# Output products of a two-block transformer kernel: tokens moved from the free axis to the partitions

## The chip, the cores and the metric

The kernel runs on one core of a Trainium2 chip (the chip has eight). The metric is the device time of one execution in microseconds, as the median of several runs. The profile shows one execution.

## What is computed

The reference runs 512 tokens of width 1024 through two blocks, all in float32. The first has two layers, each an attention mixer (first a compressed, selected and windowed one, "nsa"; then a sliding window with sinks, "swa") and a squared-ReLU MLP of 4096 hidden units. The second has a hybrid of pooling and gated linear attention ("hyb"), a cross attention to 256 memory tokens ("cross") and a convolutional gated MLP of 2816 hidden units ("ffn"). Cut to what matters here:

```python
for i in range(2):                                  # first block
    h = modulate(rms_norm(x, norm_g[i, 0]), sh1, sc1)
    y = mixer_i(h) @ w_out                          # [512, 1024] @ [1024, 1024]
    x = x + (1 + g1) * rms_norm(y, norm_g[i, 1])
    h = modulate(rms_norm(x, norm_g[i, 2]), sh2, sc2)
    y = squared_relu(h @ w_up) @ w_down             # 1024 -> 4096 -> 1024
    x = x + (1 + g2) * rms_norm(y, norm_g[i, 3])
x = x + hybrid(rms_norm(x)) @ w_out                 # second block
x = x + cross_attention(rms_norm(x), rms_norm(mem)) @ wo
x = x + (silu(gate) * val) @ w_down                 # gate, val: conv of rms_norm(x) @ w_up
return rms_norm(x)
```

The changed products are those into the model's width: `w_out`, `w_down` and `wo`, seven places in all, and the norms that follow each.

## The kernel before, in words

Every large product is made of three matmuls in a reduced float32 format. `split` (line 99) writes a high part by an ACT copy and the remainder by a subtraction on VectorE (DVE); `mm3` (L126) adds high by high, low by high and high by low. `wload` (L112) loads 512 KB of weights into one of three staging tiles `st` over the SyncE queue, splits them (`wh` on L100, `wl` on L101), and has 4 buffers of each part.

Activations lie feature by feature: x, y, h and the mixers' outputs `a` are eight chunks of 128 features in the partitions, by 512 tokens in the free axis. A product takes a 128x128 block of weights as the stationary operand, and the tokens move, 512 at once or a half of 256 (`HALVES`).

Each of the seven places ends in a *tail* (`tail`, L870): for the first half of the tokens the eight output chunks m are computed, then for the second half in the order 7 to 0. Chunks 5 to 7 keep their split weights; the other five are loaded and split a second time, so that a tail loads 13 weight tiles. Tails of the first block (`y_tail`: nsa, mlp0, swa, mlp1) write y and end in `residual` (L858); those of the second (`x_tail`: hyb, cross, ffn) add into x. The sum of squares of a token runs across partitions: `Ssq` squares each chunk on ACT, adds chunks on DVE or GpSimd (POOL) by a plan written by hand (`PA`, `PB`), and `reduce` (L292) sums over the partitions by matmuls with a column of ones. `rstd` (L244) turns two columns of sums into 1/rms, and `spread` (L261, L262) copies these over the partitions by matmuls. `residual` then does, for each of eight chunks, a scaling by the norm (L864), an addition to x (L865, on DVE and POOL in turn) and a second sum of squares, and `norm_chunk` (L323 to L328) writes the next stage's h.

What covers a tail's norms: those of the first half of the tokens run beside the second half's matmuls; those of the second beside the next stage's matmuls on the first half (`project_halves` for the MLPs, `project` with `keep=4` for swa, hyb, cross and ffn). In the two MLPs of the first block, `mem_keys` or `mem_values` (192 matmuls of 256 columns, or 96 of 512) stands in between. Of the MLP's four groups of 1024 hidden units, three go down without a tail: 8 chunks of 24 matmuls with all 512 tokens. The ffn goes down in groups of 8, 7 and 7 chunks of hidden units.

The order of instructions on each engine is not the program's: the framework schedules it when the kernel is built, by a simulated timeline, and on the chip each engine then runs its own list in order. PSUM has eight banks: four tagged `mm`, two `t`, two `o`.

## Time and profile before

| | |
|---|---|
| median of 3 runs (lowest to highest) | 2091.39 us (2090.79 to 2096.15) |
| the profiled execution | 2096.53 us |
| its span, first to last instruction | 2094.7 us |
| TensorE matmuls (PE) busy | 2019.6 us, 96% |
| weight loads into TensorE (PEld) busy | 1704.9 us, 81% |
| DVE, ACT, POOL busy | 1268.1, 925.7, 397.6 us |
| mean granted TensorE clock | 0.980 |
| moved by DMA | 265.98 MB, 127 GB/s |

A busy PE in these tables counts a matmul from its start to a modelled end, and the matmuls overlap; how fast they follow one another is read from counts over a stretch of time. "Busy" shares are averages over stages with different limits.

### The profile page before, as it was taken

How to read it: one execution, taken by the hardware profiler on the slowest of the kernel's cores; microseconds unless marked ns; L12 is line 12 of the kernel's file. 1: busy time of each engine (PE TensorE's matmuls, PEld its weight loads, DVE VectorE, ACT ScalarE, POOL GpSimd, SP SyncE). 2: the span in 40 equal slices, each digit the busy share in tenths (PEclk: the TensorE clock that was granted, in tenths of full speed). 3: DMA queues.
4: the chain of work that ended last, by engine and by line, in shares of the span. 5: the costliest groups of instructions: out<-in, count | busy, mean ns of one | idle time of the engine just before them, and what ended most of it. 6: DMA issues, size and time to landing. Idle time of an engine off the chain costs nothing.

```text
span 2094.7 us, 30152 instructions
## 1 busy us (share of the span) xinstructions
PE 2019.6 (96%) x11378; PEld 1704.9 (81%) x11378; DVE 1268.1 (61%) x2417; ACT 925.7 (44%) x1728; POOL 397.6 (19%) x328
## 2 busy tenths in 40 slices
PE   8989999989999998989899999999999999999998
PEld 7766665878888898867888888988899898888888
DVE  6778866675455568685742333587637576444455
ACT  5356566543323245455543232454545455333344
POOL 0302121131202126410421020263010001001010
PEclk9999999989999999999999999999999999999999
DMA  7675332525566554441323333443324243332333
GB/s 295 192 222 150 106 103 58 192 81 192 170 196 209 178 162 139 127 110 51 112 81 100 91 101 96 136 131 91 101 92 138 64 133 101 97 95 82 109 93 102
DMA packets 87218, 265.98 MB, mean 127 GB/s; under 512 B 13729, under 2 KB 18785, under 8 KB 87074
## 3 DMA queue, kind: packets, MB, share of 16 engines
q1 hardware_dynamic: 83970, 258.88, 39.6%
q10 hardware_dynamic: 1856, 2.59, 0.5%
q0 software_dynamic: 1248, 2.59, 0.5%
q8 instruction: 90, 1.47, 0.3%
q14 instruction: 54, 0.44, 0.1%
HBM read 240.49 MB, written 5.77 MB: 118 GB/s over the span
## 4 chain that ended last, share of the span: by engine, by line
PE 85%; DVE 8%; DMA 3%; ACT 2%; issue 2%; SPq 0%; ACTq 0%; POOL 0%; DVEq 0%; POOLq 0%
PE mm L130 23%; PE mm L129 23%; PE mm L131 23%; PE o L762 4%; PE t L446 3%; DVE wl L101 1%; DVE x L865 1%; DVE ntr L864 1%; PE mm L746 1%; PE o L352 1%; PE mm L747 1%; PE o L1005 1%; PE t L292 1%; DVE hL L328 1%; DVE ssqbV L315 1%
## 5 line engine op out<-in xcount | busy, mean ns | idle before, releaser
L100 ACT ACTIVATE wh<-st 128x1024 fp32r<-128x1024 f32 (+1 forms) x344 | 357.9, 1047 | 594.1 <-PE mm L130 513.2
L101 DVE TENSOR_TENSOR wl<-st,wh 128x1024 fp32r<-128x1024 f32 (+1 forms) x303 | 371.2, 1229 | 329.4 <-ACT wh L100 324.4
L130 PE MATMUL mm<-hL,wh 128*128 128x512 f32 (+1 forms) x1568 | 553.8, 355 | 5.2 <-DVE hL L328 5.1
L131 PE MATMUL mm<-hH,wl 128*128 128x512 f32 (+1 forms) x1568 | 551.1, 354 | 1.4 <-DVE wl L101 1.4
L129 PE MATMUL mm<-hH,wh 128*128 128x512 f32 (+1 forms) x1568 | 549.6, 356 | 2.1 <-ACT hH L100 0.9
L129 PE MATMUL mm<-aH,wh 128*128 128x256 f32 (+1 forms) x1272 | 411.8, 327 | 3.4 <-ACT wh L100 1.3
L131 PE MATMUL mm<-aH,wl 128*128 128x256 f32 (+1 forms) x1272 | 413.0, 326 | 0.6 <-DVE wl L101 0.6
L130 PE MATMUL mm<-aL,wh 128*128 128x256 f32 (+1 forms) x1272 | 413.4, 326 | 0.1
L130 PEld LDWEIGHTS mm<-hL,wh 128*128 128x128 f32 x1568 | 301.6, 193 | 45.2 <-DVE hL L328 6.2
L131 PEld LDWEIGHTS mm<-hH,wl 128*128 128x128 f32 x1568 | 301.1, 193 | 40.5 <-DVE wl L101 2.0
L129 PEld LDWEIGHTS mm<-hH,wh 128*128 128x128 f32 x1568 | 299.8, 193 | 42.0 <-ACT hH L100 1.6
L129 PEld LDWEIGHTS mm<-aH,wh 128*128 128x128 f32 x1272 | 240.0, 189 | 26.2 <-ACT wh L100 2.1
L131 PEld LDWEIGHTS mm<-aH,wl 128*128 128x128 f32 x1272 | 240.8, 189 | 21.6 <-DVE wl L101 1.2
L130 PEld LDWEIGHTS mm<-aL,wh 128*128 128x128 f32 x1272 | 241.1, 190 | 20.8 <-DVE aL L101 0.3
L928 POOL TENSOR_TENSOR relu<-relu 128x512 f32<-128x512 f32 (+1 forms) x78 | 102.3, 1318 | 494.2 <-ACT relu L923 478.2
L344 DVE SCALAR_TENSOR_TENSOR ad<-ad,cs 128x1024 f32<-128x1024 f32 x90 | 115.3, 1285 | 53.6 <-DMA ad<-in_ada_w_dram 53.5
L101 POOL TENSOR_TENSOR wl<-st,wh 128x1024 fp32r<-128x1024 f32 (+1 forms) x39 | 96.0, 2464 | 146.4 <-ACT wh L100 125.8
L446 PEld LDWEIGHTS t<-pack,P 128*128 128x128 f32 x436 | 46.9, 140 | 53.7 <-issue 49.8
L1342 POOL TENSOR_TENSOR fu<-fu 128x512 f32<-128x512 f32 x22 | 29.3, 1333 | 289.1 <-DVE fu L1336 287.9
L751 ACT ACTIVATE P<-P,m 128x128 f32<-128x128 f32 (+3 forms) x128 | 70.9, 556 | 29.8 <-DVE m L749 28.6
L100 ACT ACTIVATE aH<-relu 128x512 fp32r<-128x512 f32 (+1 forms) x78 | 43.1, 553 | 91.5 <-POOL relu L928 91.2
L762 PE MATMUL o<-PT,VV 128*64 128x512 f32 (+3 forms) x256 | 81.0, 454 | 0.6 <-ACT PT L441 0.6
(403 smaller groups left out, 2665.6 us busy)
## 6 DMA issues: line engine op xcount, KB each, us to landing
ad<-in_ada_w_dram SPq DMA_DIRECT2D x90, 512.0 KB, 4.6
st<-in_w_down_dram SPq DMA_DIRECT2D x74, 512.0 KB, 3.6
st<-in_w_up_dram SPq DMA_DIRECT2D x64, 512.0 KB, 3.6
st<-in_w_fup_dram SPq DMA_DIRECT2D x44, 512.0 KB, 3.6
st<-in_w_fdown_dram SPq DMA_DIRECT2D x21, 448.0 KB, 3.4
st<-in_w_nsa_dram SPq DMA_DIRECT2D x16, 512.0 KB, 9.5
st<-in_w_nsa_out_dram SPq DMA_DIRECT2D x13, 512.0 KB, 4.2
st<-in_w_swa_out_dram SPq DMA_DIRECT2D x13, 512.0 KB, 4.8
```

Source lines behind the costliest of these rows:

```text
L100: S.activation(h, src, AF.Copy)
L101: eng.tensor_tensor(l, src, f(h), op=OP.subtract)
L129: T.matmul(o, ah, bh, start=start and i == 0, stop=False, **kw)
L130: T.matmul(o, ah, bl, start=False, stop=False, **kw)
L131: T.matmul(o, al, bh, start=False, stop=stop and i == n - 1, **kw)
L292: T.matmul(self.v[:, tb:tb + 1], kc(q, tb), ones, start=first and tb == 0, stop=self.left < 2, skip_group_check=True)
L344: V.scalar_tensor_tensor(w, w, 1.0, cs, op0=OP.mult, op1=OP.mult, accum_out=mod[:, j:j + 1])
L446: T.transpose(o, i, ident[:n, :n] if n < 128 else ident)
L751: S.activation(pq, pq, AF.Exp, bias=m[:, qb:qb + 1], scale=-1.0, accum_out=d[:, qb:qb + 1])
L762: T.matmul(o[64 * u:64 * u + 64], vs[u], ps_[u], start=start, stop=stop, skip_group_check=True)
L928: G.tensor_tensor(r, r, r, op=OP.mult)
L1342: G.tensor_tensor(u, u, pend[0], op=OP.mult)
```

## The change

In the seven places (and in the groups that go down without a tail) the operands change places: a block of 128 tokens of `a` is stationary, and 512 columns of the weights move. Outputs, x and y have tokens in the partitions: four blocks tb of 128 tokens by 1024 features, each as two widths n of 512. A weight tile now holds 256 rows by 512 columns.

- `rows` (for groups without a tail, and for the MLPs' tails) goes over width, weight tile and the four token blocks, with banks `mm` for the first width and `o`, `o`, `t`, `t` for the second.
- `rows_last` (tails of nsa, swa, hyb, cross, ffn) does both widths for blocks 0 and 1 and keeps all its weight tiles (8, in ffn 6), then block 2, then block 3 from the kept tiles.
- The sum of squares of a token is now along the free axis: `mean_sq` gets it from ACT's accumulator, `rcol` makes 1/rms as a column, and the norm's factor is a scalar per partition. The coefficient of y, which varies along the free axis now, is copied over the partitions once for each tail by `along_rows`.
- `norm_T` brings the normed x back to features in the partitions: a matmul of each 128x128 block of x with a diagonal matrix of 1/rms, then the scale and shift on evacuation, and the split.
- `project_halves` and `project(keep=4)` take the first half of the tokens chunk by chunk, the second with k outermost (before: the other way round in `project`, and k outermost in both halves of `project_halves`).
- `wload` has 5 buffers of each part; the first five weight tiles of the program no longer have staging tiles of their own. The ffn's groups are 8, 8 and 6. Pools are opened anew for each tail. The output is stored by tokens. Weights and memory are laid out to suit on the host, as other arrangements of the same arrays.

Gone are `rms_bcast`, `Ssq`, `norm_chunk`, `norm_to_h`, `residual`, `tail`, `y_tail` and `x_tail`. The core of the diff:

```diff
+NW = 5
+NB = 'AVAVAVAV'
...
+        p_, bufs = (wp, NW) if extra is None else extra
...
+            steps = [(k, i) for k in range(nk) for i in range(n)]
+            if hi == 0:
+                steps.sort(key=lambda s: s[1])
+            for k, i in steps:
+                mm3(pieces[i], [(kc(ws[i][0], k), kc(ws[i][1], k), h[0][k][:, c], h[1][k][:, c])],
+                    start=k == 0 and i % 2 == 0, stop=k == nk - 1, skip_group_check=True)
...
+            for i in range(keep):
+                mm3(banks[i][:, HALVES[0]], chunk_terms(ws[i], h, HALVES[0], range(nk)))
             for k in range(nk):
                 for i in range(keep):
-                    c = HALVES[0]
+                    c = HALVES[1]
                     w = ws[i]
                     mm3(banks[i][:, c], [(kc(w[0], k), kc(w[1], k), h[0][k][:, c], h[1][k][:, c])], start=k == 0,
                         stop=k == nk - 1)
-            for i in range(keep):
-                mm3(banks[i][:, HALVES[1]], chunk_terms(ws[i], h, HALVES[1], range(nk)))
...
+    def rcol(v, n):
...
+        s, r = (tmp(k, [128, 4], bufs=4)[:, :n] for k in ("rc_s", "rc_r"))
+        S.activation(s, v, AF.Sqrt, bias=eps)
+        V.reciprocal(r, s)
+        V.scalar_tensor_tensor(s, r, -0.5, r, op0=OP.mult, op1=OP.mult)
+        V.scalar_tensor_tensor(s, v, 1e-6, s, op0=OP.add, op1=OP.mult)
+        V.scalar_tensor_tensor(r, s, 1.5, r, op0=OP.add, op1=OP.mult)
+        return r
...
+    def mean_sq(src, acc):
...
+        q = p.tile([128, 1024], F32, name=tag, tag=tag, bufs=bufs)[:, :src.shape[-1]]
+        S.activation(q, src, AF.Square, scale=1 / 32, accum_out=acc)
...
+    def norm_T(xs, Rs, h, c, a, b=None):
...
+        ds, w = [], 128 * len(xs)
+        for r in Rs:
+            d = tmp("diag", [128, 128], bufs=4)
+            V.tensor_scalar(d, ident, r, None, op0=OP.mult)
+            ds.append(d)
+        nb = 512 // w
+        for m0 in range(0, 8, nb):
+            o = mm("t")
+            for u in range(nb):
+                for i, x in enumerate(xs):
+                    T.matmul(o[:, u * w + i * 128:u * w + i * 128 + 128], kc(x, m0 + u), ds[i], start=True, stop=True)
...
+            for u in range(nb):
+                m = m0 + u
+                hh, hl, v, g = h[0][m][:, c], h[1][m][:, c], kc(o, u, w), a[:, m:m + 1]
+                if b is None:
+                    S.activation(hh, v, AF.Copy, scale=g)
+                    V.scalar_tensor_tensor(hl, v, g, f(hh), op0=OP.mult, op1=OP.subtract)
                 else:
...
+                    t = tmp("nt", [128, 256], bufs=3)[:, :w]
+                    if NB[m] == "A":
+                        S.activation(t, v, AF.Identity, bias=b[:, m:m + 1], scale=g)
+                    else:
+                        V.tensor_scalar(t, v, g, b[:, m:m + 1], op0=OP.mult, op1=OP.add)
+                    split(hh, hl, t)
...
+    def along_rows(col, t):
...
+        for u in range(2):
+            o = mm("t")
+            for m in range(4):
+                T.matmul(kc(o, m), col[:, 4 * u + m:4 * u + m + 1].to_broadcast([128, 128]), ident, start=True, stop=True)
+            S.activation(t[:, u * 512:u * 512 + 512], o, AF.Copy)
+        return t
...
-            stage = None if i < 3 else fp.tile([128, 1024], F32, name="st0", tag="st0", bufs=FIRST - 3)
-            first_w.append(wload(A["w_nsa"][i], stage=stage, extra=None if i < 4 else (fp, FIRST - 4)))
+            first_w.append(wload(A["w_nsa"][i]))
...
+    def row_terms(a, w, k, u, tb):
+        return [(kc(a[0][k], tb), kc(a[1][k], tb), kc(w[0], u, 512), kc(w[1], u, 512))]
+
+    def rows(src, a, nk, evac, done=None):
...
+        for n in range(2):
+            banks = [mm() for _ in range(4)] if n == 0 else [mm("o"), mm("o"), mm("t"), mm("t")]
+            for j in range(nk // 2):
+                w = wload(src(n, j))
+                steps = [(u, tb) for u in range(2) for tb in range(4)]
+                if j == nk // 2 - 1:
+                    steps.sort(key=lambda s: s[1])
+                for u, tb in steps:
+                    k = 2 * j + u
+                    mm3(banks[tb], row_terms(a, w, k, u, tb), start=k == 0, stop=k == nk - 1)
+            for tb in range(4):
+                evac(tb, n, banks[tb])
+                if n and done and tb % 2:
+                    done((tb - 1, tb))
+
+    def rows_last(src, a, nk, evac, done):
...
+        ws, nj, wx = {}, nk // 2, later[0]
+        banks = [[mm(), mm()] for _ in range(2)]
+        for n in range(2):
+            for j in range(nj):
+                w = ws[n, j] = wload(src(n, j), extra=(wx, 2 * nj - NW) if len(ws) >= NW else None)
+                steps = [(u, tb) for u in range(2) for tb in range(2)]
+                if j == nj - 1:
+                    steps.sort(key=lambda s: s[1])
+                for u, tb in steps:
+                    k = 2 * j + u
+                    mm3(banks[n][tb], row_terms(a, w, k, u, tb), start=k == 0, stop=k == nk - 1)
+            for tb in range(2):
+                evac(tb, n, banks[n][tb])
+        done((0, 1))
+        for tb in (2, 3):
+            for n in range(2):
+                o = mm("o")
+                for k in range(nk):
+                    mm3(o, row_terms(a, ws[n, k // 2], k, k % 2, tb), start=k == 0, stop=k == nk - 1)
+                evac(tb, n, o)
+            done((tb,))
...
+    def total(s):
+        V.tensor_tensor(s[:, 2:3], s[:, 0:1], s[:, 1:2], op=OP.add)
+        return rcol(s[:, 2:3], 1)
...
+    WIDTHS = [(slice(0, 512)), (slice(512, 1024))]
...
+    def y_last(how, src, a, nk, y, acc, x, h, cy, an, bn):
...
+        cb = along_rows(cy, tmp("along", [128, 1024], bufs=1))
+        ss = [small4() for _ in range(4)]
+
+        def evac(tb, n, o):
+            c = WIDTHS[n]
+            if not acc:
+                mean_sq(o, ss[tb][:, n:n + 1])
+                V.tensor_tensor(y[:, tb, c], o, cb[:, c], op=OP.mult)
             else:
...
+                V.tensor_tensor(y[:, tb, c], y[:, tb, c], o, op=OP.add)
+                mean_sq(y[:, tb, c], ss[tb][:, n:n + 1])
+                V.tensor_tensor(y[:, tb, c], y[:, tb, c], cb[:, c], op=OP.mult)
+
...
+        def done(tbs):
+            s2 = []
+            for tb in tbs:
+                r = total(ss[tb])
+                s2.append(small4())
+                for n, c in enumerate(WIDTHS):
+                    V.scalar_tensor_tensor(x[:, tb, c], y[:, tb, c], r, x[:, tb, c], op0=OP.mult, op1=OP.add)
+                    mean_sq(x[:, tb, c], s2[-1][:, n:n + 1])
+            norm_T([x[:, tb] for tb in tbs], [total(s) for s in s2], h, cols_of(tbs), an(), bn())
+        how(src, a, nk, evac, done)
...
+    def x_last(src, a, nk, x, then):
...
+        ss = [small4() for _ in range(4)]
+
+        def evac(tb, n, o):
+            c = WIDTHS[n]
+            V.tensor_tensor(x[:, tb, c], x[:, tb, c], o, op=OP.add)
+            mean_sq(x[:, tb, c], ss[tb][:, n:n + 1])
+        rows_last(src, a, nk, evac, lambda tbs: then(tbs, [total(ss[tb]) for tb in tbs]))
...
+                    with tail_pool():
+                        mem_norm(p, mh)
...
+                    cy = need(l, 5)
+                    with tail_pool():
+                        y_last(rows, src, a, 8, y, True, x, hn, cy, an, bn)
+                        mem(mp, mh)
...
-    GROUPS = ((0, 8), (8, 7), (15, 7))
+    GROUPS = ((0, 8), (8, 8), (16, 6))
...
+            if f0 < 16:
+                def add(tb, n, o):
+                    c = slice(n * 512, n * 512 + 512)
+                    V.tensor_tensor(x[:, tb, c], x[:, tb, c], o, op=OP.add)
+                rows(src, (ah, al), n, add)
             else:
-                x_tail(src, (ah, al), n, x, then, PF)
+                x_last(src, (ah, al), n, x, then)
...
+            cy = need(0, 2)
+            y = p.tile([128, 4, 1024], F32, name="y", tag="y", bufs=1)
+            with tail_pool():
+                y_last(rows_last, out_of("w_nsa_out"), a, 8, y, False, x, h, cy, lambda: need(0, 4), lambda: need(0, 3))
...
+        with pool("ffn") as p, tail_pool():
+            fw = along_rows(nw["final"], tmp("along", [128, 1024], bufs=1))
```

`y_last` and `x_last` are called from `whole` with `rows_last`, and from `mlp` with `rows`; `mem_norm` uses `mean_sq`, `rcol` and `norm_T`.

## Rows read from the trace of the kernel before

**Rows 1.** The page: busy time of each engine; shares of the chain by engine.
```profile
PE 2019.6 (96%) x11378; PEld 1704.9 (81%) x11378; DVE 1268.1 (61%) x2417; ACT 925.7 (44%) x1728; POOL 397.6 (19%) x328
...
PE 85%; DVE 8%; DMA 3%; ACT 2%; issue 2%; SPq 0%; ACTq 0%; POOL 0%; DVEq 0%; POOLq 0%
```

**Rows 2.** Windows without waits: length, then each engine’s busy us (instructions), PE clock, DMA.
```profile
510.00:740.00 230.00, 230.00 (x1016) 190.57 (x1015) 127.53 (x171) 70.41 (x89) 33.38 (x21) 1.00 0.60 194
...
379.00:400.00 21.00, 21.00 (x177) 21.00 (x177) 16.34 (x24) 9.46 (x19) 1.34 (x1) 1.00 0.97 359
```

**Rows 3.** The same view, four stretches around the ends of tails.
```profile
424.00:452.00 28.00, 17.93 (x98) 16.44 (x99) 24.06 (x47) 11.84 (x26) 12.78 (x10) 0.66 0.36 114
...
793.00:806.00 13.00, 9.89 (x81) 9.52 (x80) 12.66 (x17) 6.82 (x12) 9.99 (x6) 1.00 0.42 135
...
824.00:838.00 14.00, 10.19 (x76) 9.81 (x75) 12.78 (x22) 7.39 (x15) 5.95 (x5) 0.92 0.48 145
...
1012.00:1027.00 15.00, 9.13 (x59) 8.46 (x58) 13.15 (x24) 8.01 (x17) 5.25 (x3) 0.77 0.61 189
```

**Rows 4.** Longest waits of PE: 376 to 460, 760 to 860, 980 to 1060.
```profile
PE mm L130 <- DVE hL L328: 2.1, 1, 2.1
...
PE t L292 <- DVE ssqbV L315: 6.3, 2, 3.5
...
PE t L292 <- ACT sqP L307: 2.8, 1, 2.8
```

**Rows 5.** Groups by line and form: count, busy us, mean ns, idle before.
```profile
L101 DVE TENSOR_TENSOR wl<-st,wh 128x1024 fp32r<-128x1024 f32 x282 | 348.9, 1241 | 308.9 <-ACT wh L100 304.0 <-PE mm L131 4.4
...
L100 ACT ACTIVATE wh<-st 128x1024 fp32r<-128x1024 f32 x320 | 336.3, 1057 | 558.6 <-PE mm L130 480.9 <-DMA Z<-P 12.5 <-PE mm L131 9.7
...
L864 DVE SCALAR_TENSOR_TENSOR ntr<-y,coef,t 128x256 f32<-128x256 f32 x64 | 27.0, 474 | 3.6 <-PE t L262 3.6
...
L865 DVE TENSOR_TENSOR x<-x,ntr 128x256 f32<-128x256 f32 x32 | 27.6, 872 | 0.0
...
L315 DVE TENSOR_TENSOR ssqaV<-ssqaV,sqV 128x256 f32<-128x256 f32 x69 | 43.3, 628 | 13.7 <-ACT sqV L307 13.4
...
L328 DVE SCALAR_TENSOR_TENSOR hL<-nt,mod,hH 128x256 fp32r<-128x256 f32 x48 | 29.4, 631 | 0.6 <-ACT hH L327 0.5
...
L948 DVE TENSOR_TENSOR y<-y,mm 128x512 f32<-128x512 f32 x32 | 21.9, 686 | 71.7 <-PE mm L131 71.7
...
L946 ACT ACTIVATE y<-mm 128x512 f32<-128x512 f32 x16 | 9.2, 578 | 0.0
...
L751 ACT ACTIVATION_READ_ACCUMULATOR P<-P,m 128x1 f32 x128 | 24.2, 189 | 0.0
...
L254 DVE SCALAR_TENSOR_TENSOR rs_s<-rs_h 128x2 f32<-128x2 f32 x26 | 9.6, 374 | 0.6
```

**Rows 6.** The chain, 1498 to 1512 and 228 to 240: start, us, what.
```profile
1498.51 1.79 PE mm L1186 x16
...
230.94 1.02 PE t L446 x8
```

**Rows 7.** Windows over the span for L292 alone, then for L261 alone.
```profile
0.00:2095.00 2095.00, 23.41 (x164) 23.55 (x164) 0.98 0.41 127
...
0.00:2095.00 2095.00, 16.98 (x64) 13.06 (x64) 0.98 0.41 127
```

**Rows 8.** Line L865: duration ns min/median/max of its DVE instructions.
```profile
L865 DVE TENSOR_TENSOR x<-x,ntr x32: 410/952/2616, 411.9 to 1413.2; 128x256 f32<-128x256 f32 x32
```

**Rows 9.** DMA issues: the page; then 0 to 70 us: KB, us to landing.
```profile
st<-in_w_nsa_out_dram SPq DMA_DIRECT2D x13, 512.0 KB, 4.2
...
st<-in_w_nsa_dram SPq DMA_DIRECT2D x8, 512.0 KB, 10.2
```

**Rows 10.** Timeline of the end, DVE and the output’s DMA queue.
```profile
2084.58 0.42 DVE L909 TENSOR_TENSOR x<-x,mm 128x256 f32<-128x256 f32 x1 [1.15 <-PE mm L131]
...
2089.11 2.12 SPq L1439 DMA_DIRECT2D out_dram<-fin  x4
```

More of the change, by code (lines that the diff above doesn't have):

```diff
@@ L38 @@
 PG = ((0,), (1, 3), (2,))
-RT = "too"
 SG, SG1 = (0, 1), (0, 1)
@@ L110, in bg, with wload @@
             bg_queue.pop(0)()
[L112 to L114 removed]
+    def wload(src, n=1024, eng=V, extra=None):
+        st = wp.tile([128, 1024], F32, name="st", tag="st", bufs=3)
+        p_, bufs = (wp, NW) if extra is None else extra
         h = p_.tile([128, 1024], F32R, name="wh", tag="wh", bufs=bufs)
@@ L262, in spread, with tail_pool @@
         T.matmul(o, rl[:, j:j + 1].to_broadcast([128, 128]), identr, start=False, stop=True)
-    def rms_bcast(ssq, tag="t"):
-        rh, rl = rstd(ssq.v[:, :2], 2)
-        R = mm(tag)
-        for tb in range(2):
-            spread(kc(R, tb), rh, rl, tb)
-        return R[:, :256]
-    later = []
+    later, sq_pool = [None], [None]
+    @contextmanager
+    def tail_pool():
+        with pool("tail") as later[0]:
+            yield
     def tmp(tag, shape, dt=F32, bufs=2):
         return later[0].tile(shape, dt, name=tag, tag=tag, bufs=bufs)
-    SB, SQ, NT, NTR = {"a": 1, "b": 1}, 1, 3, 6
@@ L384, in mem_norm @@
     def mem_norm(p, mh):
-        sq = Ssq()
-        ts = []
+        ts, rs = [], []
         for i in range(2):
-            t = p.tile([128, 1024], F32, name="memt", tag="relu", bufs=3)
-            Q.dma_start(t, A["memT"][:, 4 * i:4 * i + 4].rearrange("p a t -> p (a t)"))
-            ts += [kc(t, m, 256) for m in range(4)]
-        for m in range(8):
-            sq.add(ts[m])
-        norm_to_h(ts, rms_bcast(sq), mh, slice(0, 256), nw["mem"])
+            t = p.tile([128, 1024], F32, name="relu", tag="relu", bufs=NR)
+            Q.dma_start(t, A["mem"][i])
+            ss = tmp("ss", [128, 4], bufs=12)
+            mean_sq(t, ss[:, :1])
+            ts.append(t)
+            rs.append(rcol(ss[:, :1], 1))
+        norm_T(ts, rs, mh, slice(0, 256), nw["mem"])
     def mem_keys(p, mh):
@@ L870, in tail @@
-    def tail(src, a, nk, each, after, j0=0):
-        held = {}
-        for hi, c in enumerate(HALVES):
-            for m in (range(8) if hi == 0 else reversed(range(8))):
-                w = held.pop(m) if m in held else wload(src(m), nk * 128, eng=G if (hi, m) in TG else V)
-                if hi == 0 and m >= 5:
-                    held[m] = w
-                b = mm(cols=256)
-                mm3(b, chunk_terms(w, a, c, range(nk)))
-                each(hi, c, m, b)
-            after(hi, c)
+    def row_terms(a, w, k, u, tb):
+        return [(kc(a[0][k], tb), kc(a[1][k], tb), kc(w[0], u, 512), kc(w[1], u, 512))]
@@ L1364, in whole, with to_h, out_of @@
         xp = ctx.enter_context(pool("x"))
-        later.append(xp)
-        x = xp.tile([128, 8, 512], F32, name="x", tag="x")
+        x = xp.tile([128, 4, 1024], F32, name="x", tag="x")
+        def to_h(hn, w):
+            return lambda tbs, rs: norm_T([x[:, tb] for tb in tbs], rs, hn, cols_of(tbs), w)
+        def out_of(name):
+            return lambda n, j: A[name][n, j]
         with pool("mlp0") as p, pool("mlp0_a") as pa:
-            ada_pool[:] = [p, 3, "relu"]
+            ada_pool[:] = [p, NR, "relu"]
+            sq_pool[0] = p, "relu", NR
             a = ([], [])
-            y = p.tile([128, 8, 512], F32, name="y", tag="y", bufs=1)
             for m in range(6):
@@ L1407, in whole @@
             h = hn
-        def to_h(hn, w):
-            return lambda c, R: norm_to_h([x[:, m, c] for m in range(8)], R, hn, c, w)
-        with pool("hyb") as p:
+        sq_pool[0] = None
+        with pool("hyb_a") as pa:
             a = ([], [])
-            hybrid(h, p, a)
+            with pool("hyb") as p:
+                hybrid(h, p, pa, a)
             h = new_h()
-            x_tail(lambda m: A["w_hyb_out"][m], a, 8, x, to_h(h, nw["xattn"]))
-        with pool("cross") as p:
+            with tail_pool():
+                x_last(out_of("w_hyb_out"), a, 8, x, to_h(h, nw["xattn"]))
@@ new lines, in whole, with finish @@
+            with tail_pool():
+                x_last(out_of("w_xo"), a, 8, x, to_h(h, nw["ffn"]))
+        with pool("ffn") as p, tail_pool():
+            fw = along_rows(nw["final"], tmp("along", [128, 1024], bufs=1))
+            def finish(tbs, rs):
+                for tb, r in zip(tbs, rs):
+                    for c in WIDTHS:
+                        V.scalar_tensor_tensor(x[:, tb, c], x[:, tb, c], r, fw[:, c], op0=OP.mult, op1=OP.mult)
+                        Q.dma_start(out[tb * 128:tb * 128 + 128, c], x[:, tb, c])
@@ L1504, in prep @@
     rows = np.concatenate([(g * 4 + k) * 64 + np.arange(64) for k in range(4) for g in range(4)])
-    A["w_nsa_out"] = chunks(i["nsa_w_out"][0][rows])
+    A["w_nsa_out"] = halves(i["nsa_w_out"][0][rows])
     A["cmp_pe"] = i["nsa_cmp_pe"][0].reshape(2, 2, 16, 64).transpose(1, 3, 0, 2).reshape(128, 2, 16)
@@ L1521, in prep @@
     A["w_up"] = np.concatenate([chunks(w) for w in i["mlp_w_up"]])
-    A["w_down"] = np.concatenate([chunks(w[g * 1024:(g + 1) * 1024]) for w in i["mlp_w_down"] for g in range(4)])
+    A["w_down"] = np.stack([halves(w[g * 1024:(g + 1) * 1024]) for w in i["mlp_w_down"] for g in range(4)])
     ws = i["swa_w_in"][0]
```

248 lines of the change are left out of this document (70 added, 178 removed).

## The prediction

> **What bounds the kernel now.** I read the page first: PE is busy 96% of the span and makes 85% of the chain, DVE 8% [rows 1]. So the time is TensorE's, and two things can change it: how many matmuls follow one another at which pace, and where PE stands still. Busy time cannot tell these apart, since it counts overlapping matmuls; so I took windows in which nothing waits. From 510 to 740 us all matmuls have 512 columns; the count takes in the two that straddle the edges, which leaves 1014 in 230 us, 0.2268 us each. From 379 to 400 all have 256: 175 in 21 us, 0.1200 us each [rows 2]. Two narrow ones cost 0.2400, one wide one 0.2268: a narrow pair pays 0.0132 us more for the same columns.
>
> Then I looked for PE's gaps, at the ends of tails. At the narrow pace the 98 matmuls from 424 to 452 need 11.8 us of 28: 16.2 lost, at a granted clock of 0.66, which mixes the two levels of 1.2 and 2.4 GHz. In the same way 81 matmuls leave 3.3 lost of 13 us, 76 leave 4.9 of 14, and 59 leave 7.9 of 15 [rows 3]. Sum 32.3 us: the first window is the nsa tail, the next two mlp0's, the last swa's. The waits name DVE or ACT's squares as the last to come: a late hL, sums of squares that the matmuls with ones wait for [rows 4]. In the first window DVE is busy 24.06 us of 28, so there it is the bound behind PE [rows 3]. Part of its load is contention: the addition on L865 takes 0.41 us at best and 0.95 in the median, while POOL does the same work beside it [rows 8].
>
> **The change, part by part.** *Merging.* A tail does 8 chunks x 8 k x 3 terms x 2 halves = 384 narrow matmuls; six tails and ffn's 8 x 7 x 3 x 2 = 336 make 2640. They become 1320 wide ones, the shift of a chunk of hidden units between ffn's groups included. 1320 x 0.0132 = 17.4 us less [rows 2]. The groups without a tail keep 192 wide matmuls, 24 per weight tile.
>
> The Trainium skill, page "TensorE: Matmul & The Clock Gate", section "Back-to-back issue gap", gives 262 cycles for 256 columns and 518 for 512 at full clock, so that merging a pair would save 2.5 ns; by that the 1320 pairs would give an estimated 3.3 us, not 17.4. The trace disagrees: its pair differs by 13.2 ns [rows 2].
>
> *Small matmuls.* Gone: 164 with a column of ones, and three quarters of the 64 + 64 that spread 1/rms (the gated attention keeps 16 + 16), 96 [rows 7]. New: `norm_T`, 32 for each of six tails and 16 for each of two memory norms, 224, and `along_rows`, 5 x 8 = 40. A float32 matmul of 128 columns takes 1.79/16 = 0.112 us [rows 6], so the new ones cost 29.6. The old ones: 164 between 0.112 and 0.143 (23.41/164), 96 at 0.112: 29.1 to 34.2. Net +0.5 to -4.6; I take 0, since ones in a wait cost nothing.
>
> The skill's page "Perfetto Trace Analysis", section "Transposes", speaks against `norm_T`: a transposition should use TensorE's transpose, not a standard matmul. Here standard ones take 0.112 us and the attention's transposes 1.02/8 = 0.128 [rows 6], so the trace does not bear a price out, and 224 of them would cost nothing extra.
>
> *Weights.* Tails load 8 tiles instead of 13, ffn 6 instead of 13: 37 fewer, each 1.06 us of ACT, 1.24 of DVE (POOL in some) and one DMA of 512 KB (448 in ffn) [rows 5, 9]. `rows_last` uses up a tile in 12 x 0.2268 = 2.7 us in its first phase; DVE at 1.24 and ACT at 1.06 keep up, so these are worth nothing to PE there, only room on DVE beside the norms.
>
> *The norms.* For one tail of `residual` DVE had 16 scalings (0.474), 8 additions (0.872), 17 sums (0.628), 16 `nt` at the 0.474 of their like, 16 `hL` (0.631), four chains of 1/rms (about 1.5 at the mean 0.374 of their small steps, taken for all four) and 11 weight splits: 62.5 us [rows 5]. After: 8 splits 9.9; 16 operations of 512 columns at 0.686 = 11.0; 8 chains 12; 8 diagonals, not shown, between nothing and the 0.474 of a 256-column operation, say 2; for h, 12 operations of 256 columns at 0.631 and 24 of 128 at no more than 0.474, 18.9. Sum 54, or 44 if 128 columns and small steps take half. POOL loses its 8 additions and its sums altogether, so DVE's rest runs less beside it. A seventh to a third less DVE work, in fewer steps one after another.
>
> Coverage, `rows_last`: blocks 2 and 3 take 2 x 48 x 0.2268 = 21.8 us after blocks 0 and 1 are out. Their norm is some 15 us of DVE and ACT, so h's first half should stand when PE needs it. After the last matmul, block 3's chain is some 11 us: evacuation and square 0.69 + 0.77 (ACT 0.578 + 0.189), 1/rms 1.5, x 1.4, square 0.77, 1/rms 1.5, diagonal 0.4, h 8 x 0.474 [rows 5]. The next stage's first half covers it: 7 x 24 x 0.12 = 20.2 us in the MLPs, 4 x 24 x 0.12 = 11.5 in hyb and cross. If that cover were gone it would cost 11 us a tail. `rows`: in the MLPs' tails all four blocks end within the last 4 us, so both norms, some 35 us of DVE, come after; 23 us of `mem_keys` and 11.5 of swa's first half stand over them. There I expect waits to remain.
>
> How much of the 32.3 us goes? Nothing, if the scheduled places of the new matmuls are as early as the old ones' were; all, if DVE's room decides. I take three quarters, 24 us: DVE was nearly full where PE waited [rows 3], a sixth to a third of its work goes, and waits shrink by more than the work does.
>
> *The end.* The last output's addition starts at 2084.6 and the span ends at 2094.7; the four stores are issued from 2089.1 over 2.12 us, so the end stands some 3.5 us behind the last issue [rows 10]. After: 0.69 + 0.77 + 1.5 + 2 x 0.69 + 0.6 for handing on + 3.5 = 8.4 us in place of 10.1: 1.7 less.
>
> *Start and buffers.* Without staging of their own, the fourth and fifth weight loads wait on SyncE for a split; the loads there land 10.2 us after issue [rows 9], so a queue stands before the DMA engines that hides some 4 us of blocking. 0; if that cover were gone, those 4 us. A fifth buffer: 0 to a few us of gain in the nsa stage; 0. `mean_sq` borrows a `relu` buffer in the MLPs, where ada's loads stand in line too: at most one DVE step of 1024 columns, 1.24 us [rows 5], on no path.
>
> **The sum.** -17.4 + 0 - 24 - 1.7 = -43 us. The profiled execution took 2096.5, which gives 2053.5; it lies 5.1 us above the median of the runs shown, so against that median: 2048 us.
>
> **The rivals.** *Waits unchanged:* the diagonal matmuls stand in PE's list where the ones and spreads stood, and each waits for DVE the same way. For it: most of PE's named waits are at such matmuls [rows 4]. Against: DVE's smaller load. 2091.4 - 17.4 - 1.7 = 2072 us.
>
> *No waits left:* the 32.3 us and smaller ones that I did not add up, some 10, all go: 2091.4 - 17.4 - 1.7 - 42 = 2030 us. Against it: the MLPs' tails.
>
> *The MLPs' tails eat it:* 35 us of DVE at the contended pace, 0.95 for 0.41 [rows 8], would be past 60, and each of two tails would wait some 20 us in place of 4.1 (mlp0's 8.2 over two). With three quarters of the other 24.1 gone: -17.4 - 1.7 - 18 + 40 - 8.2 = -5, 2086 us, no change. Against: POOL is busy for only part of that stretch, 5.95 us of 14 in the later window [rows 3].
>
> *Slower, by held weights:* `rows_last` holds all its tiles until block 3 has used them, and the next stage's splits are put behind block 3's norm on DVE. Then PE waits 11 + 1.06 + 1.24 = 13.3 us at each of four tails (nsa, swa, hyb, cross), where it waited 24 in all: -17.4 - 1.7 - 24 + 53 = +10, 2101 us. It decides from 10.8 us a tail. Against it: the tiles of the first width come free from 9.5 us before the end, one every 1.36.
>
> *The merge gives nothing:* if wide matmuls with a new stationary block each go at two narrow ones' pace, 0.240, the time is 2048 + 17.4 = 2065. Against: the wide ones of now have a new block each too [rows 2]. By the skill's page above it would be an estimated 2062.
>
> **How the numbers follow.** Chances: my sum 0.52, waits unchanged 0.20, none left 0.15, the MLPs' tails 0.05, held weights 0.06, merge 0.02. The range of 2024 to 2078 takes in the first three with their bounds and the last, and leaves out the tails' and the held weights' cases and some of the edges. Within 0.3% (6 us) is about what a measurement of this kernel cannot tell from no change. Faster: 0.52 + 0.20 + 0.15 + 0.02 = 0.89; same 0.05; slower 0.06. The likeliest case alone: 2040 to 2058.
>
> **What would show it.** The tails' matmuls at 0.2268 us, and 13 x 512 KB down to 8 for each weight. No window of 28 us with 16 lost behind the nsa tail. PE's waits at `norm_T`'s matmuls and at hL, in the MLPs' tails most. DVE's instructions of 0.95 gone. The prediction is wrong if PE waits for `wl` at the start of the stages after `rows_last`, or if the lost time behind the tails sums to over 20 us again.

## The result, and the profile after

The changed kernel takes 2126.6 us (median; 2125.3 to 2130.0) where the kernel before took 2091.1: ratio 1.017, 95% interval 1.0146 to 1.0193. It is 35 us slower; 43 us faster was forecast. The profiled execution took 2125.3 us, its span is 2123.2 (before 2094.7), so the two traces have 28.5 us between them.

The page of the changed kernel: span, busy times, chain by engine.

```profile
span 2123.2 us, 27619 instructions
...
PE 2035.6 (96%) x10326; PEld 1666.9 (79%) x10326; DVE 1161.2 (55%) x2322; ACT 905.3 (43%) x1740; POOL 306.4 (14%) x243
...
PE 86%; DVE 6%; ACT 3%; DMA 3%; issue 2%; ACTq 0%; SPq 0%; DVEq 0%; POOL 0%
```

Against [rows 1] DVE has 107 us less to do and POOL 91 less, as the change promised; PE has 1052 records fewer and is busy 16 us longer. What grew on PE is seen by groups, PE alone, forms apart:

```profile
L433 PE MATMUL t<-pack,P 128*128 128x128 f32 x436 | 75.7, 289 | 2.3 <-DVE PT L430 0.8 <-ACT PT L428 0.6 <-POOL P L532 0.4
...
L298 PE MATMUL t<-diag,x 128*128 128x128 f32 x384 | 52.0, 285 | 9.9 <-DVE diag L291 9.9
...
L318 PE MATMUL t<-pack,coef 128*128 128x128 f32 x64 | 8.8, 281 | 0.0
L298 PE MATMUL t<-diag,relu 128*128 128x128 f32 x64 | 8.4, 274 | 0.0
```

`norm_T`'s L298 stands with 384 + 64 = 448 records, and the program issues 224 such matmuls; `along_rows`'s L318 has 64 and, for the norms' weights, 16 (not shown) for 40. **A float32 matmul is two records**, each 0.112 us from its start to the next. The prediction counted the new ones by instructions and the old ones by records. The line that it took the price from holds the same pair: L1186's 16 records in 1.79 us [rows 6] are 8 matmuls of the program (`heads`), so 0.224 us each.

Stage by stage, from the first matmul of a stage to the first of the next (worked out from the starts of PE's matmuls in the two traces):

| stage | before | after |
|---|---|---|
| nsa; its tail | 376.4; 59.0 | 380.6; 49.3 |
| mlp0, first group; rest and tail | 56.0; 347.3 | 63.4; 345.6 |
| **swa**; its tail | **114.5**; 68.4 | **127.5**; 69.3 |
| mlp1, first group; rest and tail | 54.8; 336.2 | 56.6; 342.0 |
| hyb; its tail | 137.1; 46.3 | 130.4; 48.5 |
| cross; its tail | 66.7; 53.5 | 70.8; 56.9 |
| **ffn, first up group**; rest | **89.6**; 288.9 | **99.2**; 282.9 |

Of the four tails that stand alone only nsa's is shorter, by 9.7 us, and the group behind it loses 7.4 of these again: before, PE stood mostly ahead of that group's first matmul (435.4 us), now it stands inside the group. The greatest losses are in two stages *behind* a tail, swa and ffn's first group. PE's waits in the changed kernel (total us, times, longest):

```profile
PE mm L124 <- ACT wh L95: 14.6, 4, 10.1
PE t L298 <- DVE diag L291: 9.9, 4, 3.7
PE mm L124 <- ACT vf L1089: 6.4, 1, 6.4
PE o L124 <- DVE y L914: 4.8, 1, 4.8
PE mm L1060 <- DMA hq<-rBL: 4.7, 1, 4.7
...
PE mm L124 <- DVE fu L1369: 3.8, 1, 3.8
```

The first stands at 445 us in mlp0's first group (10.1 of the 14.6), the third at 865 in swa, the fourth at 1014 in swa's tail, the last one shown at 1769 in ffn. None of these four is at `norm_T`, where I expected them; [rows 4] had named hL and sums of squares. The waits for `diag` are at `norm_T`, in the two MLPs' tails; with those for `wh`, which stand at the starts of mlp0 and mlp1, they make 24.5 us. Windows (length, each engine's busy us, PE clock): two inside tails, then the wait of 445, what follows the one of 865, and the one of 1014.

```profile
386.00:416.00 30.00, 30.00 (x132) 24.53 (x131) 9.02 (x31) 8.69 (x24) 0.00 (x0) 1.00 0.01 4
...
2083.00:2113.00 30.00, 30.00 (x131) 24.10 (x130) 13.91 (x32) 8.87 (x21) 1.29 (x1) 1.00 0.13 48
...
442.00:457.00 15.00, 3.92 (x30) 3.43 (x28) 11.19 (x27) 9.19 (x23) 4.20 (x5) 0.77 0.32 106
...
872.20:877.30 5.10, 5.10 (x15) 3.96 (x13) 5.10 (x7) 1.02 (x2) 3.26 (x2) 0.55 0.72 201
...
1013.00:1020.00 7.00, 2.17 (x8) 1.44 (x7) 5.75 (x23) 4.59 (x15) 0.00 (x0) 0.76 0.01 4
```

The end, DVE's last block:

```profile
2115.93 0.69 DVE L937 TENSOR_TENSOR x<-x,o 128x512 f32<-128x512 f32 x1 [3.50 <-PE o L126]
...
2118.77 1.42 DVE L1471 SCALAR_TENSOR_TENSOR x<-x,rc_r,along 128x512 f32<-128x512 f32 x2
```

From 2115.9 to 2123.2 it takes 7.3 us, where [rows 10] had 10.1.

### The profile page after: what moved, and what is told of

Its sections match the earlier page's. It is cut to its first block, busy times and chain, and to the rows that moved or that the text cites. A ratio compares the mean times of both kernels' runs of the same rounds, so it can differ in the third digit from the quotient of the medians.

```text
span 2123.2 us, 27619 instructions
## 1 busy us (share of the span) xinstructions
PE 2035.6 (96%) x10326; PEld 1666.9 (79%) x10326; DVE 1161.2 (55%) x2322; ACT 905.3 (43%) x1740; POOL 306.4 (14%) x243
## 4 chain that ended last, share of the span: by engine, by line
PE 86%; DVE 6%; ACT 3%; DMA 3%; issue 2%; ACTq 0%; SPq 0%; DVEq 0%; POOL 0%
PE mm L124 18%; PE mm L126 18%; PE mm L125 18%; PE o L124 4%; PE o L125 4%; PE o L126 4%; PE o L748 3%; PE t L433 3%; PE t L298 2%; DMA ad<-in_ada_w_dram 2%; PE t L124 2%; PE t L125 2%; PE t L126 2%; PE mm L732 1%; ACT wh L95 1%
## 5 line engine op out<-in xcount | busy, mean ns | idle before, releaser
L96 DVE TENSOR_TENSOR wl<-st,wh 128x1024 fp32r<-128x1024 f32 x273 | 341.2, 1254 | 455.2 <-ACT wh L95 454.6
L95 ACT ACTIVATE wh<-st 128x1024 fp32r<-128x1024 f32 x307 | 320.8, 1053 | 554.4 <-PE mm L125 248.2
L124 PE MATMUL mm<-hH,wh 128*128 128x512 f32 (+1 forms) x1456 | 523.4, 361 | 25.7 <-ACT wh L95 14.6
L124 PE MATMUL mm<-wh,aH 128*128 128x512 f32 x444 | 173.9, 393 | 3.9 <-ACT aH L95 3.9
L125 PE MATMUL mm<-wl,aH 128*128 128x512 f32 x444 | 174.2, 392 | 0.0
L126 PE MATMUL mm<-wh,aL 128*128 128x512 f32 x444 | 171.9, 392 | 0.0
L124 PE MATMUL o<-wh,aH 128*128 128x512 f32 x284 | 113.1, 398 | 4.8 <-DVE y L914 4.8
L125 PE MATMUL o<-wl,aH 128*128 128x512 f32 x284 | 113.0, 398 | 0.0
L126 PE MATMUL o<-wh,aL 128*128 128x512 f32 x284 | 112.2, 395 | 0.0
L124 PEld LDWEIGHTS mm<-wh,aH 128*128 128x128 f32 x444 | 83.5, 188 | 22.2 <-ACT aH L95 4.1
L126 PEld LDWEIGHTS mm<-wh,aL 128*128 128x128 f32 x444 | 83.6, 188 | 18.1
```

The costliest lines, as they stand in the source:

```text
L95: S.activation(h, src, AF.Copy)
L96: eng.tensor_tensor(l, src, f(h), op=OP.subtract)
L124: T.matmul(o, ah, bh, start=start and i == 0, stop=False, **kw)
L125: T.matmul(o, ah, bl, start=False, stop=False, **kw)
L126: T.matmul(o, al, bh, start=False, stop=stop and i == n - 1, **kw)
```

## The experiments

All times are medians, "before" is the kernel before, run beside each; ratios are against it, with 95% intervals. Edits are to the changed kernel unless said. Two limits hold for all of them. In these sessions the kernel before took 2089.4 to 2093.6 us, so a difference of under some 4 us between two experiments says nothing. And each edit makes the framework schedule the whole program anew: the time to the first matmul of nsa's tail, ahead of every edit, is 376.8 to 386.5 us in the experiments' traces, so that one trace's stage shows a cause only where a wait comes or goes with it.

**1. `project`'s old order of steps.** The kernel before with the new order, and the changed kernel with the old one:

```diff
+            for k in range(nk):
+                for i in range(keep):
+                    c = HALVES[0]
...
-            for i in range(keep):
-                mm3(banks[i][:, HALVES[0]], chunk_terms(ws[i], h, HALVES[0], range(nk)))
-            for k in range(nk):
-                for i in range(keep):
-                    c = HALVES[1]
...
+            for i in range(keep):
+                mm3(banks[i][:, HALVES[1]], chunk_terms(ws[i], h, HALVES[1], range(nk)))
```

> The changed kernel with one piece put back: in `project` with held weights (swa's, cross's and ffn's first four chunks) the first half of the tokens goes k by k over all four chunks and the second half chunk by chunk, as before the change. Theory 1 (the change's new order lets all four chunks end at once, so that their banks and weights come free together: PE stands 6.7 us at 865 us and 5.1 at 885 in swa, 2.8 in cross, 3.9 in ffn's first group, and runs at the lower clock behind each): 10 to 20 us less than the changed kernel's 2126.6, so 2106 to 2117. Rival (the second half of h comes so late after the new tails that the old order waits for it instead): within 4 us of 2126.6, with new waits for hH or hL in those stages.

> The kernel before with one piece of the change: `project` with held weights takes the first half chunk by chunk and the second half k by k over all four. Theory 1 (this order lets banks and weights come free all at once, whatever the tail in front): 8 to 20 us more than 2091, so 2099 to 2111, with a PE gap of several us behind the four chunks in swa and in ffn's first group. Rival (the gap comes from the new tails in front, not from the order): 2088 to 2095.

Measured 2107.2 us (1.008; 1.0058 to 1.0101), 19.4 less, and in the kernel before 2113.7 (1.0108; 1.0081 to 1.0135), 22 more. Both go as theory 1 has it, the second 3 us beyond its range. In the first one's trace swa takes 116.6 us and ffn's first up group 93.7, which is 10.9 and 5.5 less. Waits of PE in the kernel before with that one edit:

```profile
PE mm L129 <- ACT vf L1056: 6.4, 1, 6.4
...
PE mm L129 <- DVE fu L1336: 3.8, 1, 3.8
```

They are the 6.4 and 3.8 us of the changed kernel, with the old tails in front. With k outermost in the second half the four chunks end together; their banks, and the weights for the next chunks, come free only then. That the order is a loss by itself is shown; that ending together is all of the reason is not (see the mixed order in experiment 7).

**2. Transposes for diagonal matmuls.**

```diff
-            V.tensor_scalar(d, ident, r, None, op0=OP.mult)
+            S.activation(d, s, AF.Copy, scale=Rs[i])   # or V.tensor_scalar, in turn; s: 256 columns of x
...
-                    T.matmul(o[...], kc(x, m0 + u), ds[i], start=True, stop=True)
+                    transpose(o[...], chunk(i, m0 + u))
```

> The changed kernel with norm_T's diagonal matmuls replaced: each block of x is multiplied by its 1/rms first (pieces of 256 columns, ACT and VectorE in turn), and TensorE's transpose turns it. Theory 1 (each of the 224 float32 matmuls of norm_T stands in the trace as two records of 0.112 us and costs 0.224; a transpose is one record of about 0.10): 224 x 0.12 = 27 us less for PE, of which some 5 are lost again to the 64 scalings of 256 columns, so 2100 to 2112. Rival (the small matmuls stand in waits and cost nothing, the loss is all in waits): 2122 to 2135, the scalings lengthen the chains.

2099.7 us (1.0042; 1.0024 to 1.0059), 26.9 less, 0.3 us past the near end of theory 1's range. The 224 are one record each now:

```profile
L441 PE MATMUL t<-pack,xn 128*128 128x128 f32 x224 | 34.7, 279 | 10.9 <-DVE nt L318 5.4 <-DVE rc_s L278 4.2 <-DVE xn L298 1.0
```

**3. Every diagonal matmul twice** (`for _ in range(2):` around it).

> The changed kernel with every diagonal matmul of norm_T issued twice into the same place. Theory 1 (0.224 us each, on PE's path): 224 x 0.224 = 50 us more, less what falls into waits, so 2162 to 2178. Rival (0.112 each, as the prediction had it): 25 more at the most, 2140 to 2152. Rival (they stand in waits): under 10 more.

2159.4 us (1.0323; 1.0298 to 1.0348): 32.8 more. That lies between the first two expectations: above the 25 that 0.112 us each could cost, and short of the 50 of 0.224. Its trace, of the longest of its five runs, has 448 records more (50.2 us at 0.112) and a span 45.1 us longer; some of them fall into waits. By its interval the median alone does not exclude 25. With the run before, and with the starts in the changed kernel's trace (448 records at a mean distance of 0.111 us for 224 matmuls), the price is 0.224.

**4. Squares in a buffer of their own, 5. other places for weights, 6. other banks.**

```diff
-        p, tag, bufs = sq_pool[0] or (later[0], "sq", 1)
+            q = later[0].tile([128, 512], F32, name="sq", tag="sq", bufs=1)
```

> The changed kernel with the 512-column squares of mean_sq in a buffer of their own (in the tail's pool), so that ada's loads no longer share the three relu buffers with them. Theory A for the 10.4 us that PE stands at 445 us, in the stage behind the nsa tail (ada's seven loads, held up by the squares, put their products on VectorE into the middle of block 3's norm): ada's loads go back into the tail and that stage loses 5 to 10 us, so 2116 to 2122. Theory B (PE waits there for three weights whose place in memory was the tail's pool, so that their splits stand behind the whole norm): the gap stays, 2123 to 2130.

```diff
+            lastw[0] = es.enter_context(pool("lastw")) if last else None
...
-        ws, nj, wx = {}, nk // 2, later[0]
+        ws, nj, wx = {}, nk // 2, lastw[0] or later[0]
```

> The changed kernel with the three last weights of rows_last in a pool of their own, opened ahead of the tail's other temporaries, in the two tails that an MLP follows. The three extra weights of the MLP's first stage then lie where those weights lay, and not on the norm's temporaries. Theory B (those three weights' splits wait for the last reader of the tail's pool): they go ahead of block 3's norm, the gap of 10.4 us at 445 us goes, and so do the 2.3 and 1.7 us at 1051: 8 to 16 us less, 2111 to 2119. Theory A (VectorE's ada products): within 4 us of 2126.6.

```diff
-                o = mm("o")
+                o = mm("o") if tb == 2 else mm()
```

> The changed kernel with block 3's sums in rows_last in the four banks of the first blocks, and only block 2's in the two others. Theory (the 5.2 us that PE stands at 1014 us, in the swa tail, is block 3's first matmul waiting for the bank of block 2, whose reader on VectorE stands behind the norm of blocks 0 and 1): the gap goes, 3 to 7 us less, 2120 to 2124. Rival (PE waits a little later for the same norm instead): 2125 to 2131.

(`ada` stands for the products that make the modulation's coefficients; they are computed for the most part on DVE, from weights of their own.) Squares: 2110.9 us (1.0095; 1.0073 to 1.0118), 15.7 less, more than expected; mlp0's first group loses 6.8. Places: 2114.5 (1.0106; 1.0083 to 1.0128), 12.2 less; that group loses 7.8. So both theories on the 10.1 us at 445 hold in part: each remedy closes most of that wait, and neither theory's claim that the other's remedy does nothing holds. ACT's timeline shows the second. In the changed kernel the splits of the weights that PE waits for stand behind the last reader of block 3's norm:

```profile
444.27 0.46 ACT L308 ACTIVATE nt<-t,mod,coef 128x128 f32<-128x128 f32 x1 [2.69 <-PE t L298]
...
453.65 0.31 ACT L95 ACTIVATE hH<-nt 128x128 fp32r<-128x128 f32 x1 [0.53 <-DVE nt L310]
453.87 0.40 ACT L95 ACTIVATE aH<-relu 128x256 fp32r<-128x256 f32 x1
454.17 1.99 ACT L95 ACTIVATE wh<-st 128x1024 fp32r<-128x1024 f32 x2
```

With the weights in other places they go ahead of it, 20 us earlier:

```profile
433.70 2.94 ACT L95 ACTIVATE wh<-st 128x1024 fp32r<-128x1024 f32 x3
436.55 0.28 ACT L276 ACTIVATE rc_s<-ss,eps 128x1 f32<-128x1 f32 x1
436.98 0.46 ACT L310 ACTIVATE nt<-t,mod,coef 128x128 f32<-128x128 f32 x1 [0.16 <-PE t L300]
```

The rest of the squares' gain lies mostly in swa, 127.5 to 121.2 us, where the wait for `hq` falls from 4.7 to 2.5; why is open. Banks: 2119.3 (1.0127; 1.01 to 1.0154), 7.3 less, though the intervals still touch; the wait for `y` L914 is gone, and swa's tail falls from 69.3 to 62.9 us, of which the first group of mlp1 takes 2.4 back.

**7. Remedies together:** the old order with transposes; then all five; then all five with a mixed order (second half k by k up to k = 4, then chunk by chunk); then all five with `project_halves` k by k in its first half too (its `steps.sort` left out).

> The old order of `project` with held weights and the transposes together (the first and second experiments). If the two causes are separate, their gains add up: 2126.6 - 19.4 - 26.9 = 2080, 2075 to 2085, below the kernel before (2091). If the transposes' shorter stay on PE only uncovers the same waits, 2090 to 2100.

> All five remedies on the changed kernel: transposes, the old order of `project` with held weights, squares in their own buffer, rows_last's last weights in their own pool, and block 3's sums in other banks. If the causes are separate except for the two that close the same gap at 445 us: 2082.6 - 14 (to 16) - 7 = 2060, 2054 to 2068, below the kernel before by 1 to 2 per cent and near the prediction. If PE's waits only move on to the next late operand: 2070 to 2083.

> As the run with all five remedies, but `project` with held weights keeps the new order of its first half, and its second half goes k by k over four chunks only up to k = 4 and then chunk by chunk. If what counts is that the chunks end one after the other: within 4 us of that run. If the late second half of h counts too: up to 8 us faster than it.

> As the run with all five remedies, and `project_halves` (the MLPs' first seven chunks) gets back the order before the change as well: k by k over all seven chunks in the first half too. If that order needs all seven weights at its start, the stages behind the nsa and swa tails wait for splits: 3 to 10 us more than that run. If the new order there was a loss like the one of `project`: 2 to 6 us less.

Two: 2082.6 us (0.9954; 0.9939 to 0.9969), they add up. Five: 2074.4 (0.9926; 0.9911 to 0.9941), 52 less than the changed kernel, while one by one they save 82. The gap at 445 is counted twice in the 82, and PE now waits longer elsewhere: for `wh` at the start of mlp1 (6.4 us, in the changed kernel 3.4) and for `hL` at the start of mlp0:

```profile
PE mm L125 <- ACT wh L96: 6.4, 2, 5.3
PE mm L126 <- DVE hL L97: 5.8, 1, 5.8
```

Mixed: 2087.6 (0.999; 0.9979 to 1.0002), 13 worse. There the chunks end one after the other, 9 matmuls of 0.12 us apart, so ending in turn by that much is not enough, and what else in the order costs is open; PE waits 4.3 us for `vf` in swa again. Halves: 2073.7 (0.9921; 0.9905 to 0.9938), no difference, neither expectation holds.

**8. The merge alone taken back:** each wide matmul of the tails as two narrow ones; on the changed kernel, and on the one with five remedies.

```diff
+        for c in HALVES:
+            mm3(o[:, c], [t[:2] + (t[2][:, c], t[3][:, c]) for t in terms], ...)
```

> The changed kernel with the merge alone taken back: in the six tails and ffn's last group each matmul of 512 columns is issued as two of 256, 1296 more in all, at the same places. By the prediction's term (two narrow ones 0.2400 us, a wide one 0.2268): 1296 x 0.0132 = 17.1 us more than the changed kernel's 2126.6, so 2140 to 2147. Rival (a pair costs 2.5 ns more, as the page on the clock gate has it): 3 us more, 2127 to 2133.

> As the run with all five remedies (2074.4), with the merge taken back: 1296 more matmuls, each of 512 columns issued as two of 256. On the changed kernel the same edit cost 0.8 us where 17.1 were expected. Theory (what PE saves by the merge it waits for behind the tails, whose ends VectorE and ACT set): again little, 2074 to 2081. Rival (on the changed kernel the waits that the remedies took away hid the slower matmuls; without them the merge shows its worth): 10 to 17 us more, 2084 to 2092.

2127.4 us (1.0182; 1.0167 to 1.0197): 0.8 us, no measurable difference from the merged one. With the remedies 2084.3 (0.9959; 0.9940 to 0.9979) against 0.9926: 0.33%, 7 us, with intervals that touch. The price differs from place to place. The narrow kernel's window in ffn's tail, beside the changed one's 2083 to 2113 above:

```profile
2085.00:2115.00 30.00, 30.00 (x259) 30.00 (x258) 13.21 (x32) 8.21 (x20) 1.29 (x1) 1.00 0.14 54
```

By their starts, narrow ones follow one another there at 0.1172 us, wide ones at 0.2332: a pair costs 1.2 ns more, not 13.2. That is the cheapest place. Worked out in the same way from the two traces, where nothing waits at full clock, a pair costs 4.7 ns more in swa's tail, 8.1 to 9.5 in nsa's, hyb's and cross's, and 12.5 in the MLPs': 11 us over the 1296 pairs. With the remedies it is 12, of which 7 show in the time. On the changed kernel nearly all of it goes into waits and clock: distances more than 0.5 us beyond the usual one of their shape sum to 83.9 us in the changed kernel and 75.2 in its narrow version, and the mean granted clock is 0.975 against 0.982. Whether the wide matmuls bring these waits, or another schedule of the build does, is not shown.

**9. 1/rms left out of the tails**, on the same two kernels.

```diff
-        V.tensor_tensor(s[:, 2:3], s[:, 0:1], s[:, 1:2], op=OP.add)
-        return rcol(s[:, 2:3], 1)
+        return rk
```

> The changed kernel with 1/rms left out of the tails: `total` gives a constant column, so that the sum of the two squares, the root and the four small steps behind each go, twice a block; squares, scalings, diagonals and matmuls stay. Theory (PE's waits behind the tails hang on this chain): of the 46 us of waits and slow matmuls in the stages of the nsa, mlp0, swa and mlp1 tails and behind them 15 to 30 go, 2097 to 2112. Rival (they hang on the places of weights, on banks and on what stands ahead in ACT's and VectorE's lists): at most 8 go, 2118 to 2128.

> The same with the five remedies, which leave 43 us of waits and slow matmuls in those stages. Theory (with places, banks and orders mended, the chain of 1/rms is what PE waits for): 15 to 30 us less than 2074.4, 2044 to 2059, the prediction's number. Rival: at most 8 less, 2066 to 2076.

What is left out is not the 1/rms chain alone: nothing waits for the squares any more either, and these two kernels do not compute the tails' norms, so that 2048.5 being the forecast's number is chance. 2092.2 us (0.9994; 0.9975 to 1.0013), 34 less, beyond the theory's range, and 2048.5 (0.9789; 0.9751 to 0.9826), 26 less, inside it. In each, 2.0 of these are at the program's end. In the changed kernel without 1/rms the waits at `diag` are gone, those at `wh` are down to 0.4 us, and those of swa's and ffn's order stay:

```profile
PE mm L124 <- ACT vf L1090: 6.4, 1, 6.4
PE mm L1061 <- DMA hq<-rBL: 4.7, 1, 4.7
...
PE mm L124 <- DVE fu L1370: 3.8, 1, 3.8
```

**10. Links of that chain:** root and reciprocal without the refinement's three steps (`V.reciprocal(r, s)`, then `return r`); one chain for two blocks (two columns at once); both, with experiment 7's `project_halves`.

> The kernel with all five remedies, and in the tails' 1/rms the three small steps behind the reciprocal (the refinement) left out: root and reciprocal alone. Leaving out the whole chain of 1/rms took 26 us from that kernel. Theory (each link of the chain counts by its length; three of its six links, 0.17 us each with the same again in hand-over): 8 to 16 us less than 2074.4, 2058 to 2066. Rival (the sum over the squares and the hop to ACT for the root make the wait, not VectorE's small steps): at most 5 less.

> The kernel with all five remedies, and one chain of 1/rms for the two blocks of a pair (two columns at once) instead of one each: five chains fewer of each kind of norm where pairs end together. Theory (VectorE's many small steps delay what stands behind them): 3 to 8 us less than 2074.4, 2066 to 2071. Rival (the first block of a pair now waits for the second): no change or up to 5 more, 2073 to 2080.

> Both of these, with the old order of `project_halves` as well. If they add: 12 to 22 us less than 2074, 2052 to 2062, the fastest of all runs that compute the whole.

2069.9 us (0.9899; 0.9869 to 0.9928), 2072.7 (0.9915; 0.9884 to 0.9945), 2071.1 (0.9923; 0.9895 to 0.9951), against 2074.4 (0.9926): the intervals overlap. The first two fit their rivals (the second misses its by 0.3 us), and the gains do not add. The refinement is at most a small part of what PE waits for, and DVE's load is not it: without the refinement DVE is busy for 1154.9 us in place of 1183.4, 28.5 less, for 4.5 us of time; without the whole chain it is 1146.7, 36.7 less, for 26 (pages of the kernels with five remedies, without the refinement, without the chain):

```profile
PE 1999.2 (97%) x10102; PEld 1629.5 (79%) x10102; DVE 1183.4 (57%) x2350; ACT 925.6 (45%) x1796; POOL 309.9 (15%) x243
...
PE 1996.5 (97%) x10102; PEld 1626.6 (79%) x10102; DVE 1154.9 (56%) x2206; ACT 926.5 (45%) x1796; POOL 307.6 (15%) x243
...
PE 1995.5 (98%) x10102; PEld 1625.4 (79%) x10102; DVE 1146.7 (56%) x2131; ACT 911.4 (45%) x1749; POOL 309.1 (15%) x243
```

Which of the other links it is (the squares on ACT, the sum, the hop to ACT for the root) stays open.

## Why the prediction was wrong

The two spans differ by 28.5 us, where the sum said -43. Of the 71.5 between them the small matmuls make 30, the waits some 36, the merge some 6; the end goes 1 the other way.

**The small matmuls, "I take 0": this step failed.** Old ones: 164 x 0.112 + 96 x 0.112 = 29.1 us, counted in records. New ones: 264 x 0.112 = 29.6, counted in instructions, of which each has two records: 528 x 0.112 = 59.1. Net +30.0. Experiments 2 and 3 show it on the chip. The price was misread where it was taken: [rows 6] has 16 records for 8 matmuls. The Trainium skill's page "Perfetto Trace Analysis", section "Transposes", had the right of it; I set it aside by comparing one of two records (0.112) with the one record of a transpose. The Trainium skill's page "FP8 and Floating Point Precision", section "TensorE Precision Notes", says that true float32 makes four passes; the trace agrees: 0.224 us is 3.95 times the 0.0567 that 128 of the 512 columns of a wide fp32r matmul take at 0.2268.

**The waits, "three quarters of 32.3 go": this step failed too, its sign was wrong.** The spans differ by 28.5 = 30.0 for small matmuls, less 11 for the merge (experiment 8), less 2.8 at the end, plus the waits and what goes with them: some +12 in place of -24. Measured directly, by the starts as in experiment 8, the waits grew from 70.5 to 83.9 us between the two traces. One of the prediction's signs of being wrong, over 20 us lost behind the tails, is there with the 24.5 us for `wh` and `diag`; the other, a wait for `wl` at a stage's start, showed as one for `wh`. Four steps made this up:
- *"DVE's room decides."* DVE lost 8% of its work and PE still waits. Taking out the 1/rms chain, and with it the waiting for the squares, gives 34 and 26 us (experiment 9), while 28.5 us less of DVE's work give 4.5 (experiment 10): so PE waits for the chain behind a tail, not for DVE's load; which link of it, is open. I had the chain (11 us) but set it against the cover of the next stage's first half.
- *That cover.* Behind hyb's and cross's tails it held: where cross and ffn begin PE waits for nothing over 0.5 us. In mlp0 it did not, because the squares hold up ada's loads and because the stage's extra weights lie where the tail's pool was (experiments 4 and 5). That pools are opened anew stood in the diff, and I gave it no price.
- *`mean_sq` "on no path".* With a buffer of its own 15.7 us come back, 6.8 of them in mlp0's first group.
- *`project`'s order* is not in the sum at all: 19.4 us (experiment 1). My rival of held weights was of this kind, but I put it on `rows_last`'s tiles.

**The merge, -17.4: the direction was right, the size not.** The two prices came from two places, wide ones from the MLP's middle (0.2268), narrow ones from a tail. In the tails wide ones go at 0.2273 to 0.2332 and narrow ones at 0.1172 to 0.1199, which makes 11 us of the 17.4. Taken back, it is worth 0.8 us, with the remedies 7. The page "TensorE: Matmul & The Clock Gate" of the Trainium skill, section "Back-to-back issue gap", gave an estimated 3.3 us for all pairs, by a formula that it calls one for isolated matmuls; the 11 us lie between that and my 17.4.

**Right:** the end (-2.8 for -1.7); the weights (8 tiles of 512 KB for each tail, and inside the tails PE waits for no weight); less work on DVE and POOL. The MLPs' tails, a rival, did not decide: their `diag` waits are 9.9 us together, where that rival had 40.

## What to carry to other kernels

Before a count is multiplied by a duration from the trace, check that both are in the same unit: divide a line's records by the instructions that the program issues there. When DVE work is taken off behind a TensorE stage, price the longest chain from its last matmul to the next operand, and look at what lies in the same memory and in the same banks; here a smaller sum of work shortened none of these. And an order of steps that lets several chunks end together cost 19 to 22 us here and stood in no sum: undo each such reordering alone, in both kernels, for it is the cheapest test there is.

## What the runs showed of the hardware

- A float32 matmul of 128 columns stands as two records of 0.112 us; doubling 224 of them added 32.8 us to the median, and 45.1 to the span of the one execution traced, the longest of five.
- A wait cost more than its length here: behind the 6.4 us at 865 the window from 872.2 to 877.3 has a granted clock of 0.55, between the levels of 2.4 and 1.2 GHz and near the lower, and by their starts 13 wide matmuls take 0.392 us each there: 2.1 us more than at 0.2268. From 386 to 416, inside nsa's tail, where PE does not stand, it is 1.00.
- Wide matmuls of one shape follow one another at 0.2268 to 0.2332 us, narrow ones at 0.1172 to 0.1200, according to the place, so that at one and the same place a pair of narrow ones costs 1.2 to 12.5 ns more than a wide one (experiment 8). What in the place does it, no run here shows.
